# Expert mixer of a decoder layer: stored groups interleaved with direct ones, nine stored groups last, and new places for two sets of weights

## The chip, the cores and the metric

The kernel runs on one core of a Trainium2 chip. The metric is the device time of one execution in microseconds (us). A core has five engines that each work through a queue of their own in a fixed order: TensorE (PE; its weight loads are PEld), VectorE (DVE), ScalarE (ACT), GpSimd (POOL) and SyncE (SP, which only issues transfers here). Transfers of all queues run on the same 16 DMA engines.

## The reference, cut to what matters

One decoder layer for 1024 prompt tokens and 64 sample tokens, 1024 features wide: a token mixer, then an expert mixer (PEER), then a gated per-layer embedding (PLE) and a last norm. The change lies in the expert mixer and in the loading of the embedding's weights:

```python
# expert mixer: 16384 experts = 128 blocks of 128; 8 heads pick 16 experts each, so 128 per token
hval = jnp.einsum('pd,phkd->phk', xb, u_tab[e])
act = jax.nn.gelu(hval, approximate=False) * gsm
y = jnp.einsum('phk,phkd->pd', act, v_tab[e])
...
# per-layer embedding, which closes the layer
gate = jax.nn.sigmoid(rmsnorm(h, ple_norm) @ ple_gate)
h = h + gate * (p_l @ ple_proj)
```

## The kernel before

The tokens are nine tiles of 128 (the last, tile 8, holds the 64 sample tokens). The expert mixer treats them in two ways that run side by side.

**By gathers** (tiles 0, 1, 8, 2, 3; `gather`, L1161 to L1189). For each of a token's 128 experts POOL issues one indirect transfer that fetches a row of 1024 numbers per token (`grow`, 512 KB), first from the table of u, then from that of v. DVE takes each up with one instruction of 128x1024 elements: a product with the token's features and its sum for u (L1175), a weighted addition to `gacc` for v (L1189). Five buffers hold the fetched rows, so POOL can be at most five gathers ahead of DVE. There are 1152 gathers; tile 3 comes last, and its sum is added in the closing stage to the last tile's residual (L1447).

**Densely** (tiles 4 to 7, 512 tokens at once). For each block of 128 experts `hidden` loads 512 KB of u (`uraw`), splits it into a high and a low part (ACT L307, POOL L311), multiplies in 24 matmuls of 512 columns (L336, L337, L339) and applies the GELU; `act` multiplies with the gate weights (`wt`, one load of 448 KB for two blocks) and splits again (`ah`, `al`). `dense` then takes a group of blocks through eight output steps. A step loads its piece of v (`vraw`), splits it (`vh`, `vl`), does three matmuls per block into `py` (L1351, L1352, L1354) and adds the result to `yT` on DVE (L1358).

The hidden values of blocks 0 to 71 are computed in an earlier stage and stored in memory (`gd`); here they are called **stored** blocks, and the dense stage only loads them back (`ge`, 256 KB a block, two buffers). Blocks 72 to 127 are **direct**: their 24 hidden matmuls are done in the dense stage, between the steps of the group before. `dense_fused` runs the 14 direct groups of four blocks first, and `dense_stored` then the stored ones in 15 groups (14 of five blocks, one of two). While these run, `ple_weights` loads 20 pieces of the embedding's weights (`pgr`, 256 KB each, in buffers of the tag `vraw`) and splits them into the room that the tables of u have left; the last block of them has two buffers of its own (`pgx`). One piece is taken up every four steps (`PWS`).

**The closing stage** (`ple`) takes the nine tiles in the order 0, 1, 4, 5, 6, 7, 8, 2, 3: a norm, 60 matmuls with the embedding's weights, and the final norm (`fin`, L1490). Tile 3, the last, waits for the last gather.

No order is written out by hand. The code names the instructions in one sequence, with the gathers at a lower priority (`behind`), and a scheduler that models time turns it into one fixed list for each engine when the program is built. An engine never takes a later instruction of its list before an earlier one.

Of the kernel before, what the change touches and what calls it, by code (L numbers as in the profile page):

```python
# [9 lines left out]
F32 = mybir.dt.float32  # L10
F32R = mybir.dt.float32r
# [3 lines left out]
AF = mybir.ActivationFunctionType  # L15
# [149 lines left out]


CSTA = 288
NB = 5
GBUF = 5
UB = 2  # L170
PE_ = 0
# [2 lines left out]
PWS = 4  # L174
NPRE = 72
NF = 4
TK1 = {8: 0, 2: 1, 3: 4}
GEB = 2
GHB = 2
WQ = 32  # L180
VB = 4
WB = 2
AB = 8
CRING = 4
# [36 lines left out]
class K:  # L221
# [1116 lines left out]
    def dense(self, dl, dr, yT, groups, acts_of, side):  # L1338
        nc, I = self.nc, self.I
        for g0, nb in groups:  # L1340
            acts = acts_of(g0, nb)
            for d in range(8):
                next(side, None)
                raw = dl.tile([128, NB, 128], F32, name="vraw", bufs=VB)[:, :nb]
                nc.sync.dma_start(raw, I['pvd'][d, :, g0:g0 + nb])
                vh = dr.tile([128, NB, 128], F32R, name="vh")[:, :nb]
                vl = self.lo.tile([128, NB, 128], F32R, name="vl", bufs=2)[:, :nb]
                self.split(vh, vl, raw, "g")
# [9 lines left out]
                    nc.vector.tensor_tensor(yT[:, d, :], yT[:, d, :], p, op=OP.add)  # L1358
            self.first = False

    def dense_fused(self, dl, dr, hp, x, yT):

        groups = [(g, min(NF, 128 - g)) for g in range(NPRE, 128, NF)]
        made = {}

        def make(g):
            for b in range(g, min(g + NF, 128)):
                made[b] = self.act(dl, dr, b, self.hidden(hp, None, x, b))
                yield
                yield  # L1370

        for _ in make(NPRE):
            pass
        for g0, nb in groups:
            side = make(g0 + NF)
            self.dense(dl, dr, yT, [(g0, nb)], lambda g, n: [made.pop(b) for b in range(g, g + n)], side)
            for _ in side:
                pass

    def dense_stored(self, dl, dr, yT, side):  # L1380

        def acts(g0, nb):
            out = []
            for b in range(g0, g0 + nb):
                ge = dl.tile([128, self.ntok], F32, name="ge", bufs=GEB)
                self.nc.sync.dma_start(ge, self.gd[b])
                p = self.psh.tile([128, self.ntok], F32, name="ph")
                self.nc.scalar.activation(p, ge, AF.Copy)
                out.append(self.act(dl, dr, b, p))
            return out  # L1390

        def spread():
            while True:
                next(side, None)
                for _ in range(PWS):
                    yield

        self.dense(dl, dr, yT, [(g, min(NB, NPRE - g)) for g in range(0, NPRE, NB)], acts, spread())

    def ple_weights(self, cx, da, dl):  # L1400
        nc, I = self.nc, self.I
        kc = self.ntok // 128
        bufs = dict(uraw=UB, uh=DW, ul=LW, spare=1)
        names = [n for n in bufs for _ in range(bufs[n])]
        nc.sync.dma_start(self.pn, I['pnorm'])
        self.pg, self.pp = [], []
        for j in range(2):
            a = cx.tile([128, kc, 1024], F32R, name="pga", tag=f"cx{j}")
            self.pg.append([a[:, k] for k in range(kc)])
            self.pp.append([])  # L1410
# [9 lines left out]
        for w, src, n in ((self.pp, 'pproj', 2), (self.pg, 'pgate', 8)):  # L1420
            for k in range(n):
                for c in range(2):
                    cs = slice(c * 512, c * 512 + 512)
                    raw = dl.tile([128, 512], F32, name="pgr", tag="vraw", bufs=VB)
                    nc.sync.dma_start(raw, I[src][k, :, cs])
                    if src == 'pgate':
                        nc.scalar.activation(raw, raw, AF.Copy, scale=self.pn[:, k:k + 1])
                    self.split(w[0][k][:, cs], w[1][k][:, cs], raw, "g")
                    yield

    def ple(self, rp, tps, yT):
        nc, I, O = self.nc, self.I, self.O
# [3 lines left out]
        for i, t in enumerate(E0 + G2 + G1):  # L1436
# [50 lines left out]
            for c in range(2):  # L1487
                cs = slice(c * 512, c * 512 + 512)
                fin = rp.tile([128, 512], F32, name="fin", tag="vraw", bufs=VB)
                nc.vector.scalar_tensor_tensor(fin[:n], h[:n, cs], r[:n], gf[:n, cs], op0=OP.mult, op1=OP.mult)  # L1490
                nc.scalar.dma_start(O['y'][t * 128:t * 128 + n, cs], fin[:n])

    def build(self):
# [3 lines left out]
        with self.es:  # L1497
# [13 lines left out]
            a = self.group_a(pools, A0, "b", mixes)  # L1511
# [5 lines left out]
            a = self.group_a(pools, A1, "b")  # L1517
# [11 lines left out]
            a = self.group_a(self.a_pool(e2, "2"), A2, "b")  # L1529
# [4 lines left out]
            late = self.group_b(BORDER, early)  # L1534
# [10 lines left out]
            cx = sb("cx2", ex)  # L1545
            x = self.rows_of(cx, G2)
            da = sb("dna", eg, bufs=2)
# [17 lines left out]
            last = self.c_rows(co, late[-1], CRING, da, [y[:, :, n3:] for y in x])  # L1565
# [22 lines left out]
            yT = sb("dy", ey, side="right").tile([128, 8, self.ntok], F32, name="yT")  # L1588
# [3 lines left out]
            with ExitStack() as e:  # L1592
# [9 lines left out]
                for i, t in enumerate(G2 + [None]):  # L1602
                    tk = self.topk(tp, t) if t is not None else iter(())
                    while True:
                        a, b = next(tk, "end"), next(gate, "end")
# [13 lines left out]
            with ExitStack() as e:  # L1619
                dl = sb("dl", e, bufs=2)  # L1620
                with ExitStack() as e2:
                    self.psh = self.pool("psumh2", bufs=3, space=PS, es=e2, reuse_waits="tile")
                    self.ps2 = self.pool("psumy", bufs=3, space=PS, es=e2, reuse_waits="tile")
                    dr = sb("dr", e2, bufs=2)
                    self.dense_fused(dl, dr, da, x, yT)
                    self.dense_stored(dl, dr, yT, self.ple_weights(cx, da, dl))
# [23 lines left out]
```

## Time and profile before

| | |
|---|---|
| three timed runs | 3568.96, 3544.32 and 3556.01 us, median 3556.01 us |
| the profiled execution | 3571.98 us, its span 3570.2 us |
| first and last dense output matmul (`py`) | 2365.4 and 3405.2 us |
| PE busy, share of the span | 3218.4 us, 90% |
| DVE, POOL, ACT busy | 2801.1, 2330.2, 1177.6 us |
| moved by DMA | 1058.86 MB, mean 297 GB/s |

Times in rows are from the start of the span. The work before the dense stage fills about two thirds of the span. Shares of busy time are averages over stages with different limits, so the views by stretch and the waits say more than the table does.

### The profile page before, as it was taken

To read this page: it belongs to the slowest core of one execution; us is meant where nothing else is said; L and a number is where in the kernel's file an instruction comes from. 1 tells how busy PE (TensorE), PEld (TensorE's weight loads), DVE (VectorE), ACT (ScalarE), POOL (GpSimd) and SP (SyncE) were. 2 spreads that over 40 slices of the span, in tenths; PEclk is the share of its full clock that TensorE was granted. 3 is DMA by queue.
4 is the path that set the end of the run, shared out by engine and by line. 5 is a ranking of instruction groups with operands and counts; after the bars stand their busy time and mean duration, and the time that the engine had idled before them with its cause. 6 is when DMAs were issued, how large, how long until landed. Compare 5 with 4: busy or idle time off the path is not lost. (4 is left out here: it accounts for less than half of the span.)

```text
span 3570.2 us, 51592 instructions
## 1 busy us (share of the span) xinstructions
PE 3218.4 (90%) x17493; PEld 2663.8 (75%) x17493; DVE 2801.1 (78%) x5530; ACT 1177.6 (33%) x2255; POOL 2330.2 (65%) x2078
## 2 busy tenths in 40 slices
PE   7998995877869887879999999999999998899998
PEld 7897994654757666748877888878888886677775
DVE  4544589897797787879978899877777777788887
ACT  4332221111112111213235777743333333344322
POOL 5642577555345465545478787778888877788753
PEclk9999996656878787889999999999999999999999
DMA  8548599889857888896579888999999999999985
GB/s 267 173 136 272 188 314 327 274 311 323 299 179 267 286 296 277 290 351 228 196 270 311 330 323 334 345 348 343 340 344 339 341 333 371 352 377 385 343 276 203
DMA packets 416675, 1058.86 MB, mean 297 GB/s; under 512 B 45275, under 2 KB 140889, under 8 KB 411738
## 3 DMA queue, kind: packets, MB, share of 16 engines
q0 software_dynamic: 165888, 604.05, 47.2%
q1 hardware_dynamic: 198046, 364.18, 30.5%
q10 hardware_dynamic: 52476, 87.31, 6.6%
q8 instruction: 139, 2.28, 0.3%
q14 instruction: 126, 1.03, 0.1%
HBM read 968.09 MB, written 87.29 MB: 296 GB/s over the span
## 5 line engine op out<-in xcount | busy, mean ns | idle before, releaser
L1161 POOL DMA_INDIRECT grow<-in_pv,eid x576 | 566.2, 983 | 461.3 <-DVE gacc L1189 241.1
L1161 POOL DMA_INDIRECT grow<-in_pu,eid x576 | 560.8, 974 | 344.9 <-DVE grow L1175 218.4
L1175 DVE SCALAR_TENSOR_TENSOR grow<-grow,gacc 128x1024 f32<-128x1024 f32 x576 | 689.0, 1213 | 95.1 <-DMA grow<-in_pu,eid 92.5
L1189 DVE SCALAR_TENSOR_TENSOR gacc<-grow,ac,gacc 128x1024 f32<-128x1024 f32 x571 | 731.8, 1282 | 35.5 <-DMA grow<-in_pv,eid 29.1
L1351 PE MATMUL py<-ah,vh 128*128 128x512 f32 x1024 | 405.8, 397 | 23.2 <-ACT vh L307 20.9
L336 PE MATMUL ph<-cx,uh 128*128 128x512 f32 x1024 | 405.4, 396 | 6.2 <-ACT uh L307 6.1
L1352 PE MATMUL py<-al,vh 128*128 128x512 f32 x1024 | 404.7, 395 | 2.4 <-DVE al L309 2.2
L337 PE MATMUL ph<-cx,uh 128*128 128x512 f32 x1024 | 403.4, 394 | 0.0
L311 POOL TENSOR_TENSOR vl<-vraw,vh 128x512 fp32r<-128x512 f32 (+2 forms) x232 | 328.1, 1418 | 29.3 <-ACT vh L307 21.3
L311 POOL TENSOR_TENSOR ul<-uraw,uh 128x1024 fp32r<-128x1024 f32 x128 | 308.3, 2408 | 42.4 <-ACT uh L307 13.0
L1354 PE MATMUL py<-ah,vl 128*128 128x512 f32 x1024 | 278.0, 399 | 9.7 <-POOL vl L311 8.2
L339 PE MATMUL ph<-cx,ul 128*128 128x512 f32 x1024 | 263.6, 395 | 4.9 <-POOL ul L311 4.8
L1351 PEld LDWEIGHTS py<-ah,vh 128*128 128x128 f32 x1024 | 195.0, 190 | 73.6 <-ACT vh L307 28.5
L307 ACT ACTIVATE vh<-vraw 128x512 fp32r<-128x512 f32 (+2 forms) x232 | 156.0, 675 | 270.8 <-DMA vraw<-in_pvd 89.2
L1354 PEld LDWEIGHTS py<-ah,vl 128*128 128x128 f32 x1024 | 192.6, 190 | 61.1 <-POOL vl L311 17.5
L1358 DVE TENSOR_TENSOR yT<-yT,py 128x512 f32<-128x512 f32 x224 | 153.1, 684 | 105.3 <-PE py L1354 96.3
L336 PEld LDWEIGHTS ph<-cx,uh 128*128 128x128 f32 x1024 | 193.9, 189 | 49.2 <-ACT uh L307 8.9
L1352 PEld LDWEIGHTS py<-al,vh 128*128 128x128 f32 x1024 | 194.9, 190 | 45.5 <-DVE al L309 3.7
L339 PEld LDWEIGHTS ph<-cx,ul 128*128 128x128 f32 x1024 | 190.8, 189 | 44.7 <-POOL ul L311 6.8
L337 PEld LDWEIGHTS ph<-cx,uh 128*128 128x128 f32 x1024 | 193.6, 189 | 39.2
L307 ACT ACTIVATE uh<-uraw 128x1024 fp32r<-128x1024 f32 x128 | 135.0, 1055 | 158.9 <-DMA uraw<-in_puT 73.3
L311 POOL TENSOR_TENSOR wl<-wraw,wh 128x1024 fp32r<-128x1024 f32 x45 | 114.7, 2548 | 108.4 <-ACT wh L307 60.6
(420 smaller groups left out, 7041.4 us busy)
## 6 DMA issues: line engine op xcount, KB each, us to landing
uraw<-in_puT SPq DMA_DIRECT2D x128, 512.0 KB
vraw<-in_pvd SPq DMA_DIRECT2D x112, 320.0 KB
cw<-in_w_out SPq DMA_DIRECT2D x128, 256.0 KB
wd<-wst ACTq DMA_DIRECT2D x28, 1024.0 KB
wt<-wd SPq DMA_DIRECT2D x64, 448.0 KB
vraw<-in_pvd SPq DMA_DIRECT2D x112, 256.0 KB
wraw<-in_w_ret SPq DMA_DIRECT2D x48, 512.0 KB
wraw<-in_w_rw SPq DMA_DIRECT2D x42, 512.0 KB
```

The lines of the kernel that those rows point to most:

```text
L307: nc.scalar.activation(hi, src, AF.Copy)
L311: nc.gpsimd.tensor_tensor(lo, src, hi.bitcast(F32), op=OP.subtract)
L336: mm(out, lh(k), rh(k), start=first and k == 0, stop=False)
L337: mm(out, *((ll(k), rh(k)) if right else (lh(k), rl(k))), start=False, stop=False)
L339: mm(out, *((lh(k), rl(k)) if right else (ll(k), rh(k))), start=False, stop=last and k == nk - 1)
L1161: nc.gpsimd.indirect_dma_start(out=g, out_offset=None, in_=src, in_offset=bass.IndirectOffsetOnAxis(ap=self.eid[t][:, j:j + 1], axis=0))
L1175: nc.vector.scalar_tensor_tensor(g[:, c], g[:, c], 1.0, x[:, c], op0=OP.mult, op1=OP.mult, accum_out=hv[:, i, j:j + 1])
L1189: nc.vector.scalar_tensor_tensor(y[:, c], g[:, c], ac[:, j:j + 1], y[:, c], op0=OP.mult, op1=OP.add)
L1351: nc.tensor.matmul(p, vh[:, b, :], ah, start=b == 0, stop=False)
L1352: nc.tensor.matmul(p, vh[:, b, :], al, start=False, stop=False)
L1354: nc.tensor.matmul(p, vl[:, b, :], ah, start=False, stop=b == nb - 1)
L1358: nc.vector.tensor_tensor(yT[:, d, :], yT[:, d, :], p, op=OP.add)
```

## The change

The two functions become one, `dense_all`. All groups now have four blocks: 14 direct ones and 18 stored ones. The first nine stored groups are put between the direct ones (direct 72, direct 76, stored 0, direct 80, direct 84, stored 4 and so on by the first block's number); the other nine (`REST`) follow at the end. Each group's hidden values are prepared during the eight steps of the group before it, stored or direct alike. The embedding's weights are taken up during the last nine groups alone, one piece in three steps (`EVERY`). The raw loads of v get six buffers of four blocks in place of four of five. The raw weights move out of those buffers: all but the last block of them are loaded in one transfer of 512 KB into the two `pgx` buffers, one ahead, and the last block's own two tiles take that place when the raw loads have left it.

```diff
-NB = 5
+NB = 4
+REST = 9
+EVERY = 3
-VB = 4
+VB = 6
...
+    def dense_all(self, dl, dr, hp, x, yT, weights):
+        direct = list(range(NPRE, 128, NF))
+        stored = list(range(0, NPRE, NF))
+        beside = len(stored) - REST
+        order = []
+        for i, g in enumerate(direct):
+            order += [g] + stored[i * beside // len(direct):(i + 1) * beside // len(direct)]
+        order += stored[beside:]
+        made = {}
+
+        def make(g):
+            for b in range(g, g + NF):
+                if g < NPRE:
+                    ge = dl.tile([128, self.ntok], F32, name="ge", bufs=GEB)
+                    self.nc.sync.dma_start(ge, self.gd[b])
+                    h = self.psh.tile([128, self.ntok], F32, name="ph")
+                    self.nc.scalar.activation(h, ge, AF.Copy)
+                else:
+                    h = self.hidden(hp, None, x, b)
+                made[b] = self.act(dl, dr, b, h)
+                yield
+                yield
+
+        def both(a, b):
+            while True:
+                next(a, None)
+                next(b, None)
+                for _ in range(EVERY - 1):
+                    yield
+                    next(a, None)
+                yield
...
+        for i, g in enumerate(order):
+            side = make(order[i + 1]) if i + 1 < len(order) else iter(())
+            last = i >= len(order) - REST
+            self.dense(dl, dr, yT, [(g, NF)], lambda g0, nb: [made.pop(c) for c in range(g0, g0 + nb)], both(side, weights) if last else side)
+            for _ in side:
+                pass
+        for _ in weights:
+            pass
...
     def ple_weights(self, cx, da, dl):
...
-                        else:
-                            r[j].append(dl.tile([128, 1024], F32R, name="pgx", bufs=2))
...
+        def load(w, src, k):
+            if (w, k) in late:
+                raw = [dl.tile([128, 512], F32, name="pgr", tag="vraw", bufs=VB) for c in range(2)]
+                for c in range(2):
+                    nc.sync.dma_start(raw[c], I[src][k, :, c * 512:c * 512 + 512])
+            else:
+                raw = dl.tile([128, 2, 512], F32, name="pgr", tag="pgx", bufs=2)
+                nc.sync.dma_start(raw, I[src][k].rearrange("p (c d) -> p c d", c=2))
```

The lists of all engines are the same as before up to the start of the dense stage. (Two new lines of constants move the line numbers by two, and those behind `dense_all` by 24.) Three places in the lists show what moves.

On DVE, the end of the program before. `gacc` is the sum of tile 3's gathers, `fin` the last operation on a tile of the closing stage:

```order
L1482 SCALAR_TENSOR_TENSOR ph<-psg,ph 64x512
L1189 SCALAR_TENSOR_TENSOR gacc<-grow,ac,gacc 128x1024 x3
L1490 SCALAR_TENSOR_TENSOR fin<-ph,frs,row_norm_final 64x512 x2
L1481 SCALAR_TENSOR_TENSOR psg<-psg,ppp 128x512
L1189 SCALAR_TENSOR_TENSOR gacc<-grow,ac,gacc 128x1024
L1482 SCALAR_TENSOR_TENSOR ph<-psg,ph 128x512
L1189 SCALAR_TENSOR_TENSOR gacc<-grow,ac,gacc 128x1024 x2
L1447 TENSOR_TENSOR ph<-ph,gacc 128x1024
```

The same place of the changed program, from the last but one tile on:

```order
L1505 SCALAR_TENSOR_TENSOR psg<-psg,ppp 128x512
L1191 SCALAR_TENSOR_TENSOR gacc<-grow,ac,gacc 128x1024
L1506 SCALAR_TENSOR_TENSOR ph<-psg,ph 128x512
L1191 SCALAR_TENSOR_TENSOR gacc<-grow,ac,gacc 128x1024 x3
L1514 SCALAR_TENSOR_TENSOR fin<-ph,frs,row_norm_final 128x512 x2
L1191 SCALAR_TENSOR_TENSOR gacc<-grow,ac,gacc 128x1024 x42
L1471 TENSOR_TENSOR ph<-ph,gacc 128x1024
L311 TENSOR_TENSOR pxl<-ntr,pxh 128x512 x2
L1505 SCALAR_TENSOR_TENSOR psg<-psg,pyt 128x512
```

Before, the last gathers stand between the operations of tiles 8 and 2; now 42 of them stand alone between the end of tile 2 and the start of tile 3's norm.

On POOL, among the stored groups before, where `vl` is the split of v for one step, `pgb` one of the embedding's weights and `grow` a gather:

```order
L311 TENSOR_TENSOR vl_28619<-vraw_28616,vh_28618 128x640
L1161 DMA grow_21708<-in_pv,eid3_69 128x1024
L311 TENSOR_TENSOR vl_28642<-vraw_28639,vh_28641 128x640
L1161 DMA grow_21711<-in_pv,eid3_69 128x1024
L1161 DMA grow_21714<-in_pv,eid3_69 128x1024
L311 TENSOR_TENSOR pgb_26574<-pgr_28662,pgb_26573 128x512
L311 TENSOR_TENSOR vl_28670<-vraw_28667,vh_28669 128x640
L1161 DMA grow_21717<-in_pv,eid3_69 128x1024
L1161 DMA grow_21720<-in_pv,eid3_69 128x1024
L311 TENSOR_TENSOR vl_28693<-vraw_28690,vh_28692 128x640
```

And in the last nine groups of the changed program:

```order
L313 TENSOR_TENSOR vl_29114<-vraw_29111,vh_29113 128x512
L1163 DMA grow_21632<-in_pu,eid3_69 128x1024
L313 TENSOR_TENSOR vl_29139<-vraw_29136,vh_29138 128x512
L313 TENSOR_TENSOR vl_29171<-vraw_29168,vh_29170 128x512
L1163 DMA grow_21635<-in_pu,eid3_69 128x1024
L1163 DMA grow_21638<-in_pu,eid3_69 128x1024
L313 TENSOR_TENSOR vl_29191<-vraw_29188,vh_29190 128x512
L313 TENSOR_TENSOR vl_29224<-vraw_29221,vh_29223 128x512
L1163 DMA grow_21641<-in_pu,eid3_69 128x1024
```

There are fewer gathers for each step of v, and at this place tile 3 is still at its rows of u (`in_pu`) where before it was at those of v.

On SP, in the interleaved part of the changed program, before a stored group's turn (`uraw` belongs to the direct group that follows, `ge` and `wt` to the stored one and to both):

```order
L1315 DMA uraw_24272<-in_puT 128x1024
L1347 DMA vraw_23972<-in_pvd 128x512
L1347 DMA vraw_23992<-in_pvd 128x512
L1378 DMA ge_24012<-gd_15428 128x512
L1315 DMA uraw_24352<-in_puT 128x1024
L1378 DMA ge_24064<-gd_15428 128x512
L1347 DMA vraw_24024<-in_pvd 128x512
L1347 DMA vraw_24044<-in_pvd 128x512
L1331 DMA wt_24016<-wd_15427 128x7x128
L1331 DMA wt_24146<-wd_15427 128x7x128
```

Before, the direct groups' part of this list had only `uraw`, `vraw` and `wt`, and all but the first two loads of `ge` came behind it. Now loads for both kinds of block stand close together ahead of each stored group.

More of the change, by code (lines that the diff above doesn't have):

```diff
@@ L1359, in dense @@
             self.first = False
-    def dense_fused(self, dl, dr, hp, x, yT):
-        groups = [(g, min(NF, 128 - g)) for g in range(NPRE, 128, NF)]
+    def dense_all(self, dl, dr, hp, x, yT, weights):
[6 more added lines that the diff above has]
+        order += stored[beside:]
@@ L1364, in dense_fused @@
         made = {}
         def make(g):
-            for b in range(g, min(g + NF, 128)):
-                made[b] = self.act(dl, dr, b, self.hidden(hp, None, x, b))
+            for b in range(g, g + NF):
[7 more added lines that the diff above has]
+                made[b] = self.act(dl, dr, b, h)
@@ L1369, in make @@
                 yield
                 yield
-        for _ in make(NPRE):
-            pass
-        for g0, nb in groups:
-            side = make(g0 + NF)
-            self.dense(dl, dr, yT, [(g0, nb)], lambda g, n: [made.pop(b) for b in range(g, g + n)], side)
+        def both(a, b):
[6 more added lines that the diff above has]
+                yield
@@ L1377, in dense_fused @@
+        for _ in make(order[0]):
+            pass
+        for i, g in enumerate(order):
+            side = make(order[i + 1]) if i + 1 < len(order) else iter(())
+            last = i >= len(order) - REST
+            self.dense(dl, dr, yT, [(g, NF)], lambda g0, nb: [made.pop(c) for c in range(g0, g0 + nb)], both(side, weights) if last else side)
             for _ in side:
                 pass
[L1380 to L1398, printed above, removed]
+        for _ in weights:
+            pass
@@ L1417, in ple_weights @@
                             r[j].append(da.tile([128, 1024], F32R, name="pgb", tag=tag, bufs=bufs[tag]))
-                        else:
-                            r[j].append(dl.tile([128, 1024], F32R, name="pgx", bufs=2))
-        for w, src, n in ((self.pp, 'pproj', 2), (self.pg, 'pgate', 8)):
-            for k in range(n):
-                for c in range(2):
[L1423 to L1429, printed above, removed]
+        pieces = [(w, src, k) for w, src, n in ((self.pp, 'pproj', 2), (self.pg, 'pgate', 8)) for k in range(n)]
+        late = [(w, k) for w, src, k in pieces if len(w[0]) <= k]
+        raws = []
+        def load(w, src, k):
+            if (w, k) in late:
+                raw = [dl.tile([128, 512], F32, name="pgr", tag="vraw", bufs=VB) for c in range(2)]
+                for c in range(2):
+                    nc.sync.dma_start(raw[c], I[src][k, :, c * 512:c * 512 + 512])
+            else:
+                raw = dl.tile([128, 2, 512], F32, name="pgr", tag="pgx", bufs=2)
+                nc.sync.dma_start(raw, I[src][k].rearrange("p (c d) -> p c d", c=2))
+                raw = [raw[:, c] for c in range(2)]
+            raws.append(raw)
+        load(*pieces[0])
+        for i, (w, src, k) in enumerate(pieces):
+            if i + 1 < len(pieces):
+                load(*pieces[i + 1])
+            raw = raws.pop(0)
+            if (w, k) in late:
+                for j in range(2):
+                    w[j].append(dl.tile([128, 1024], F32R, name="pgx", bufs=2))
+            for c in range(2):
+                cs = slice(c * 512, c * 512 + 512)
+                if src == 'pgate':
+                    nc.scalar.activation(raw[c], raw[c], AF.Copy, scale=self.pn[:, k:k + 1])
+                self.split(w[0][k][:, cs], w[1][k][:, cs], raw[c], "g")
+                yield
     def ple(self, rp, tps, yT):
@@ L1624, in build @@
                     dr = sb("dr", e2, bufs=2)
-                    self.dense_fused(dl, dr, da, x, yT)
-                    self.dense_stored(dl, dr, yT, self.ple_weights(cx, da, dl))
+                    self.dense_all(dl, dr, da, x, yT, self.ple_weights(cx, da, dl))
                 ek.close()
```

## The prediction

> **What bounds the kernel now.** I read the busy time by stretch first: the interleaved direct part of the dense stage, its stored part, and the closing stage up to the end of the last but one tile. After the stretch and its length the columns are PE, PEld, DVE, ACT and POOL busy with counts, the granted clock, the DMA share and GB/s.
>
> ```profile
> 2365.00:2930.00 565.00, 565.00 (x2476) 464.48 (x2475) 429.62 (x614) 175.09 (x261) 479.80 (x392) 1.00 0.95 338
> 2930.00:3405.00 475.00, 439.66 (x1824) 345.50 (x1823) 384.96 (x625) 188.33 (x309) 386.13 (x326) 0.97 1.01 364
> 3405.00:3553.00 148.00, 133.51 (x612) 104.43 (x613) 120.49 (x132) 40.90 (x74) 75.65 (x93) 0.98 0.75 256
> ```
>
> and the 100 us of the stored part in which most was moved:
>
> ```profile
> 3200.00:3300.00 100.00, 94.29 (x401) 74.04 (x400) 83.04 (x119) 42.18 (x67) 83.94 (x69) 1.00 1.05 386
> ```
>
> While direct groups run, PE has no gap. While stored ones run it has, and the DMA share is at 1.01: PE has moved from bound to waiting. How much that costs comes from the pace of a full PE. The chain of waits holds one piece per hidden block while direct groups run, 33 pieces from this first to this last one; below them the first of an output step's three lines, with its first and last start:
>
> ```profile
> 2572.04 1.81 PE ph L339 x8
> ...
> 2922.76 1.81 PE ph L339 x8
> ...
> L1351 PE MATMUL py<-ah,vh x1024: 387/389/796, 2365.4 to 3404.0; 128*128 128x512 f32 x171
> ```
>
> They lie 350.72 / 32 = 10.96 us apart, and in each 10.96 us stand 24 hidden and 24 output matmuls: 0.2283 us a matmul. From 2365.4 to 3404.0 PE does 3 x 1024 output matmuls, but for the last few, and 13 direct groups x 96 hidden ones, some 4315 in all: 985 us of 1038.6. So **about 54 us** are lost, nearly all in the stored part. The waits of that part (who waited for whom: us, times, longest) say why:
>
> ```profile
> ACT vh L307 <- DMA vraw<-in_pvd: 89.2, 43, 7.2
> ...
> SPq L1345 <- POOL vl L311: 227.0, 97, 5.3
> ```
>
> The split of v, which PE needs, waits for its load, and the load's issue for one of the four buffers. The bytes agree. These are the sizes of one load:
>
> ```profile
> uraw<-in_puT SPq DMA_DIRECT2D x128, 512.0 KB
> vraw<-in_pvd SPq DMA_DIRECT2D x112, 320.0 KB
> ...
> wt<-wd SPq DMA_DIRECT2D x64, 448.0 KB
> vraw<-in_pvd SPq DMA_DIRECT2D x112, 256.0 KB
> ...
> ge<-gd SPq DMA_DIRECT2D x72, 256.0 KB
> ...
> pgr<-in_pgate SPq DMA_DIRECT2D x16, 256.0 KB
> ```
>
> The gathers come on top; by stretch (DVE and POOL busy with counts, clock, DMA share, GB/s) POOL issued 239, 175 and 53:
>
> ```profile
> 2365.00:2930.00 565.00, 296.60 (x350) 227.12 (x239) 1.00 0.95 338
> 2930.00:3405.00 475.00, 217.92 (x282) 166.93 (x175) 0.97 1.01 364
> 3405.00:3553.00 148.00, 72.67 (x57) 56.56 (x53) 0.98 0.75 256
> ```
>
> A stored group of five blocks wants 2.62 MB of v, 1.31 of `ge`, 1.15 of `wt`, 0.36 of embedding weights and 175 / 14.4 = 12.2 gathers of 0.524 MB (a row of 4 KB for 128 partitions), 11.8 MB in the 27.4 us that its 120 matmuls take: 432 GB/s, where 364 came. At 364 it takes 32.5 us, and 14.4 of them 468 of the 475 us. The stored part is bound by transfers, and more than half of these are gathers.
>
> The kernel's end hangs on the gathers too:
>
> ```profile
> 3536.33 3.94 DVE L1189 SCALAR_TENSOR_TENSOR gacc<-grow,ac,gacc 128x1024 f32<-128x1024 f32 x3 [0.97 <-DMA grow<-in_pv,eid]
> ...
> 3543.90 2.60 DVE L1189 SCALAR_TENSOR_TENSOR gacc<-grow,ac,gacc 128x1024 f32<-128x1024 f32 x2
> 3546.53 1.22 DVE L1447 TENSOR_TENSOR ph<-ph,gacc 128x1024 f32<-128x1024 f32 x1
> ...
> 3552.34 1.42 DVE L1490 SCALAR_TENSOR_TENSOR fin<-ph,frs,row_norm_final 128x512 f32<-128x512 f32 x2 [0.99 <-POOL frs L302]
> ```
>
> Tile 3's chain starts with L1447 at 3546.5, right behind the last gather, and takes the 23.7 us to 3570.2; tile 2 ends at 3553.8. So dense work and gathers end together now, and a change helps only if it shortens both.
>
> **The change part by part.** *Dense stage.* The interleaved part holds 14 direct and 9 stored groups, 807 us at PE's pace. A direct group moves 2.10 MB of u, 2.10 of v and 0.92 of `wt`; a stored one 2.10, 1.05 and 0.92. Counted in DVE's list, 302 gathers go beside them (681 stand ahead of the first addition to `yT`, 983 ahead of the 23rd group's end). That is 108 + 158 = 266 MB, 330 GB/s, below the 338 at which PE ran full. The nine last groups take 21.9 us each at PE's pace and want 4.07 MB, 0.58 of embedding weights and 66 / 9 = 7.3 gathers (3.84 MB): 8.5 MB, 388 GB/s. The best stretch above gave 386, the stored part 364; at 364 a group takes 23.3 us, a loss of 1.4 x 9 = 13 us. The short stretches before a stored group, in which PE has only output matmuls, want 7 to 10 gathers and 4.07 MB in 21.9 us, 353 to 425 GB/s. Unlike the stored part before, each stands behind a stretch of 43.8 us with less traffic, and v has six buffers for steps of 2.7 us. I put 3 us of the 54 on them. So the dense stage gives back 54 - 13 - 3 = **38 us**. Its ends are 0 (all stretches wait as the stored part did) and 54.
>
> *More steps.* Groups of four make 256 steps of the 232, so 24 more additions and splits:
>
> ```profile
> L1358 DVE TENSOR_TENSOR yT<-yT,py 128x512 f32<-128x512 f32 x224 | 153.1, 684 | 105.3 <-PE py L1354 96.3
> ```
>
> 24 x 0.684 = 16 us of DVE over 1000 us, beside PE's matmuls, whose number stays. I cost it at nothing; without the cover it would be 16 us. The weights of the embedding keep their bytes and splits, one transfer of 512 KB for two of 256 KB; nothing, as their last splits stand ahead of the last groups' end in POOL's list.
>
> *The gathers.* Fewer go beside the dense stage: behind its last addition DVE's list has 103, before 56. Five of the 47 stand among the closing stage's tiles, which PE fills to 133.5 of 148 us, at most 5 x 1.28 us; I take 2. The other **42 stand alone**, between the end of tile 2 and tile 3's chain. The trace has no such run, so I bound it. Below, DVE: three gathers back to back took 3.94 us, 1.31 each, 55 us for 42. Above, the five buffers: one is used again when its gather has landed and DVE is through, so five gathers take one landing plus 1.31 us and about 0.15 to the next issue. A short and a long landing for which DVE waited, as issue on POOL and use on DVE; the long one's use is the first row of the end above:
>
> ```profile
> 2899.12 0.96 POOL L1161 DMA_INDIRECT grow<-in_pu,eid  x1 [0.16 <-issue]
> ...
> 2903.66 1.22 DVE L1175 SCALAR_TENSOR_TENSOR grow<-grow,gacc 128x1024 f32<-128x1024 f32 x1 [1.36 <-DMA grow<-in_pu,eid]
> ...
> 3526.93 2.60 POOL L1161 DMA_INDIRECT grow<-in_pv,eid  x1 [0.17 <-DVE psg L1481]
> ```
>
> These are 4.5 and 9.4 us: (4.5 + 1.46) / 5 = 1.2, so DVE's 1.31 us a gather, or (9.4 + 1.46) / 5 = 2.2; for 42, 55 or 91 us. In the run nothing else moves and the first five have landed, so I take a value near the short row, 1.43 us, which is 367 GB/s: **60 us**. In front of it stand the 7.3 us by which tile 2 ends behind the last gather now.
>
> *PE goes cold.* After an idle gap, the matmuls of the closing stage come at this pace:
>
> ```profile
> 3419.25 1.97 PE L330 MATMUL ntr<-csta,ph 128*128 128x128 f32 x8 [3.98 <-DVE ph L1452]
> ...
> 3421.87 0.63 PE L336 MATMUL ppg<-pga,pxh 128*128 128x512 f32 x1
> 3422.30 0.63 PE L337 MATMUL ppg<-pga,pxh 128*128 128x512 f32 x1
> ```
>
> They start 0.43 us apart, near half pace, for some 5 us: 2.6 us lost. Behind the lone run tile 3 starts like that; 3 us.
>
> The sum, against the profiled execution's 3571.98 us (span 3570.2, 1.8 around it): -38 + 7 + 60 + 2 + 3 = **+34 us**, 3606. That execution is 16 us above the median of the runs, 3556.0; against the median it is 3590, 0.95% more.
>
> The Trainium skill, in DMA: Bandwidth & Descriptors, has two rules on this. Its section on the anatomy of a DMA on the GpSimd path puts one at about 2.0 us plus its bytes at 436 GB/s, 3.2 us for a gather here; the shortest row above is 4.5 us from issue to use. By that rule the lone run would go at DVE's pace, 55 us, and the sum would be +29; this is the first rival's price. Its section on specifications names about 358 GB/s from HBM for a core; by it the last groups' 8.5 MB would take 23.7 us, 16 us lost in place of 13, and the sum would be +37. The 386 GB/s row does not agree with it.
>
> **The rivals.**
>
> *The dense stage gives everything back and the run goes at DVE's pace.* -54 + 55 + 7 + 0 + 0 = +8 us, 3564: not slower. For it: 330 GB/s is under what the full PE stood, and the lone run has the DMA engines to itself. Against it: 388 GB/s in the last groups. It decides where those hold 386. 0.25.
>
> *The loads for the short stretches come late.* Four `ge` through two buffers, `wt` and the next group's u stand in one SP list with v, and the list stops at its first full buffer: 227 us of such waits stand above. If nine stretches lose 3 us each and the last groups wait like the stored part, the stage gives back 10 us, and a run at 1.6 us takes 67: -10 + 67 + 7 + 2 + 3 = +69 us, 3625, slower by 1.9%. For it: the bursts of 425 GB/s. Against it: the quieter 43.8 us ahead of each. 0.25.
>
> *Faster by over 1%* would take 36 us. PE's 54 us, and the 14.5 us that it idles in the closing stage, are less than 55 + 7 + 36. Only a gain ahead of the dense stage, where the lists are equal, could make it: 0.02. That the change does not interleave is excluded by the lists.
>
> **How the numbers follow.** Forecast (+34, from +20 to +50) 0.48, first rival 0.25, second 0.25, faster 0.02. A measurement of this kernel can tell about 1%, 36 us, from no change. The first rival and a little over half of the forecast lie within it: 0.25 + 0.27 = 0.52; the rest of the forecast and the second rival are slower: 0.21 + 0.25 = 0.46. The terms' ends give -54 + 55 + 7 = +8 to 0 + 91 + 7 + 6 + 3 = +107; a run at 2.2 us is unlikely beside idle DMA engines, so the range ends at +70, and begins at 0 for the spread of the runs: 3556 to 3626.
>
> **What would show it.** In the changed profile: no PE gap to speak of among the first 23 groups; the last output matmul about 38 us earlier, near 3367; DMA at 364 to 386 GB/s in the last nine groups; then, behind the end of tile 2, a stretch of some 60 us in which DVE does only L1191, POOL only L1163, and PE nothing; tile 3's first matmuls at half pace. I am wrong if that stretch is under 50 us, or if the gain ahead of it is over 54 or under 10.

## The result, and the profile after

The changed kernel takes 3587.94 us (median of four runs, 3581.34 to 3596.83) against 3555.71 us for the kernel before (four runs): the ratio on record is **1.0086, with a 95% interval from 1.0057 to 1.0116** (the quotient of the two medians is 1.0091). The forecast was 3590 us, in a range from 3556 to 3626. The profiled execution took 3581.34 us, its span 3579.6 us.

Busy time by stretch in the changed kernel, with the columns of the prediction: the dense stage up to the embedding's weights, while these are taken up, the last nine groups, the closing stage to the end of tile 2, and what follows up to tile 3's chain.

```profile
2347.00:3066.00 719.00, 718.52 (x3141) 589.76 (x3140) 546.35 (x841) 243.84 (x380) 596.92 (x493) 1.00 0.95 337
3066.00:3141.00 75.00, 71.42 (x305) 56.48 (x304) 56.93 (x105) 39.94 (x71) 67.82 (x61) 1.00 1.03 371
3141.00:3342.00 201.00, 197.95 (x858) 160.00 (x857) 166.34 (x273) 80.67 (x143) 163.01 (x146) 1.00 0.97 342
3342.00:3490.00 148.00, 128.03 (x587) 99.60 (x585) 125.29 (x136) 38.50 (x70) 83.38 (x101) 0.98 0.82 278
3490.00:3554.00 64.00, 0.00 (x0) 0.00 (x0) 53.93 (x42) 0.00 (x0) 35.31 (x38) 0.50 0.91 330
```

PE is full through the interleaved part (0.5 us of gaps in 719) and nearly so to the end of the dense stage. Behind the closing stage come 64 us in which PE does nothing. The wait for the loads of v, 89.2 us in the stored part before, has shrunk to this in the whole dense stage:

```profile
ACT vh L309 <- DMA vraw<-in_pvd: 4.7, 2, 2.9
```

The gathers alone, by stretch (DVE and POOL busy with counts; DVE has two instructions for a row of u, so the gathers are POOL's count): 370 issued beside the dense stage, 63 beside the closing stage, and 42 taken up by DVE behind it.

```profile
2347.00:3342.00 995.00, 456.49 (x587) 352.09 (x370) 1.00 0.96 341
3342.00:3490.00 148.00, 78.81 (x63) 64.51 (x63) 0.98 0.82 278
3490.00:3554.00 64.00, 53.93 (x42) 35.31 (x38) 0.50 0.91 330
```

The kernel's end on DVE, from the end of tile 2 to tile 3:

```profile
3488.44 1.41 DVE L1514 SCALAR_TENSOR_TENSOR fin<-ph,frs,row_norm_final 128x512 f32<-128x512 f32 x2
3489.77 3.93 DVE L1191 SCALAR_TENSOR_TENSOR gacc<-grow,ac,gacc 128x1024 f32<-128x1024 f32 x3
3494.67 1.29 DVE L1191 SCALAR_TENSOR_TENSOR gacc<-grow,ac,gacc 128x1024 f32<-128x1024 f32 x1 [0.97 <-DMA grow<-in_pv,eid]
...
3550.03 3.94 DVE L1191 SCALAR_TENSOR_TENSOR gacc<-grow,ac,gacc 128x1024 f32<-128x1024 f32 x3 [0.24 <-DMA grow<-in_pv,eid]
3554.00 1.22 DVE L1471 TENSOR_TENSOR ph<-ph,gacc 128x1024 f32<-128x1024 f32 x1
```

From 3489.8 to 3554.0 DVE does 42 additions of 1.29 us, with waits of 0.2 to 1.1 us for a gather between them: 64.2 us, 1.53 a gather. Tile 3's chain then takes 25.6 us to the span's end.

The two profiled spans differ by only 9.4 us, less than the medians do. The dense stage began 18.5 us earlier in the profile after (2346.7 against 2365.2), although all lists are equal up to there. In the seven profiles of kernels that have nothing changed ahead of it (before, after and the first five experiments below) it began anywhere from 2346.7 to 2370.5. So stages are compared from their own start here: from the first `py` (its weight load included) to the span's end 1205.0 us before and 1232.9 after, 27.9 more; the medians differ by 32.2.

### The profile page after: what moved, and what is told of

It is laid out like the page before. It is cut to its first block, busy times and chain, and to the rows that moved or that the text cites. A ratio compares the mean times of both kernels' runs of the same rounds, so it can differ in the third digit from the quotient of the medians.

```text
span 3579.6 us, 51796 instructions
## 1 busy us (share of the span) xinstructions
PE 3204.7 (90%) x17493; PEld 2661.9 (74%) x17493; DVE 2819.8 (79%) x5554; ACT 1177.7 (33%) x2279; POOL 2330.6 (65%) x2102
## 2 busy tenths in 40 slices
DMA packets 418835, 1058.86 MB, mean 296 GB/s; under 512 B 45515, under 2 KB 140105, under 8 KB 413898
## 5 line engine op out<-in xcount | busy, mean ns | idle before, releaser
L313 POOL TENSOR_TENSOR vl<-vraw,vh 128x512 fp32r<-128x512 f32 x256 | 331.7, 1300 | 61.6 <-ACT vh L309 33.5
L309 ACT ACTIVATE vh<-vraw 128x512 fp32r<-128x512 f32 x256 | 161.3, 631 | 353.8 <-PE py L1354 219.1
L1360 DVE TENSOR_TENSOR yT<-yT,py 128x512 f32<-128x512 f32 x248 | 169.7, 685 | 133.8 <-PE py L1356 132.2
L341 PEld LDWEIGHTS ph<-cx,ul 128*128 128x128 f32 x1024 | 190.1, 188 | 43.3 <-POOL ul L313 5.4
```

The source lines that it names most:

```text
L309: nc.scalar.activation(hi, src, AF.Copy)
L313: nc.gpsimd.tensor_tensor(lo, src, hi.bitcast(F32), op=OP.subtract)
L341: mm(out, *((lh(k), rl(k)) if right else (ll(k), rh(k))), start=False, stop=last and k == nk - 1)
```

## The experiments

Two theories stood against each other. **A**, the forecast's: interleaving and the deeper buffers win back PE's time in the dense stage, and the lone run of gathers takes it away again; without that run the gain is there to be had. **B**: transfers bind this half of the kernel, the sum of bytes is the same (1058.86 MB), and the dense stage became shorter mostly because its gathers were put off; the order of the groups hardly matters.

All runs in one table. "Beside" are the gathers that POOL issued from the first to the last `py`, "MB" what moved in that time (both counted in the trace), "lone" the time from the end of tile 2 to the last gather's addition, with the gathers that DVE's list has there. A dash: the gathers ended before tile 2 did. "Single run": timed once, so without a ratio. The stage times come from one profile of each kernel; the four with 362 to 371 gathers beside the dense stage and six buffers for v lie within 6 us of each other (993.9 to 999.8), so differences of that size say nothing. e9 and e10 do 72 more matmuls in the dense stage than the others (16 us, see below).

| kernel | dense us | PE gaps us | beside | MB | closing us | lone us (gathers) | ratio to before |
|---|---|---|---|---|---|---|---|
| before | 1040.2 | 35.3 | 415 | 364 | 148.1 | - | 1 |
| after | 994.9 | 7.1 | 370 | 339 | 148.0 | 64.1 (42) | 1.0086 [1.0057, 1.0116] |
| e1_without_42 | 999.8 | 10.3 | 370 | 339 | 147.1 | 1.2 (0) | 0.9913 [0.9884, 0.9942] |
| e2_four_buffers | 1042.2 | 35.3 | 395 | 352 | 150.6 | 21.7 (14) | 1.0093 [1.0053, 1.0133] |
| e3_three_buffers | 1078.5 | 60.9 | 421 | 366 | 138.3 | - | 1.0080 [1.0048, 1.0113] |
| e4_six_in_old_order | 1011.9 | 18.3 | 388 | 349 | 141.7 | 32.2 (21) | 1.0025 [0.9999, 1.0050] |
| e5_no_interleave | 1012.4 | 18.0 | 384 | 346 | 140.5 | 41.1 (27) | 1.0054 [1.0031, 1.0078] |
| e6_six_gather_buffers | 1018.7 | 19.6 | 392 | 350 | 140.5 | - | 1.0165 [1.0125, 1.0205] |
| e7_six_gather_buffers_old_order | 1106.2 | 79.8 | 424 | 370 | 131.0 | - | 1.0412 [1.0372, 1.0453] |
| e8_four_gather_buffers | 993.9 | 5.6 | 362 | 335 | 153.2 | 105.2 (58) | single run |
| e9_six_with_room_in_yT | 1040.9 | 22.9 | 400 | 359 | 141.1 | - | 1.0021 [0.9996, 1.0047] |
| e10_same_without_interleave | 1062.4 | 35.7 | 427 | 372 | 142.0 | - | 1.0040 [1.0016, 1.0065] |
| e11_one_store_buffer | 998.6 | 8.2 | 371 | 339 | 144.0 | 43.3 (28) | single run |

**e1_without_42: the lone run taken away.** The changed kernel without the last 42 of tile 3's v rows.

```diff
         y = home()
+        n = n - 42 if t == G1[-1] else n
         for j in range(n):
```

> The changed kernel without the last 42 gathers of tile 3's rows of v (their part of the sum is left out); all lists are otherwise as in the changed kernel, and no gather stands alone any more. Theory A (the dense stage gained about 45 us and the lone run takes it back and more): 3588 - 42 x 1.53 = about 3524 us, that is 32 us under the kernel before, with the last output matmul about where it is in the changed kernel. Theory C (the changed kernel is slow for another reason, such as late loads in the short stretches; the lone run only fills time that would be lost anyway): less than 40 us off, over 3548.

Measured: 3537.91 us against 3570.5 us for the kernel before, timed beside it, ratio 0.9913. Tile 3's sum lacks these rows; only the time of the run is of use. Against the change's own ratio this is 1.0086 - 0.9913 = 1.73%, 62 us, where the profile gives the lone run 64. The dense and the closing stage stayed as they were (999.8 and 147.1 us). The price of the lone run is shown; not what put it there.

**e2_four_buffers and e3_three_buffers: the buffers of v undone, the new order kept.**

```diff
-VB = 6
+VB = 4      # e3: 3
```

> The changed kernel with four raw buffers for v in place of six. In DVE's list 76 gathers are then left behind the dense stage (103 with six, 56 before) and 14 stand alone (42 with six). Theory A (interleaving leaves room, so that gathers beside the dense stage are nearly free): the lone run falls by 28 x 1.53 = 43 us, the last nine groups pay 5 to 10: about 3553 us, equal to before. Theory B (transfers are the bound everywhere, and a gather moved beside the dense stage costs its 0.524 MB at about 364 GB/s, 1.44 us, there): -43 + 27 x 1.44 = -4, about 3584 us.

> The changed kernel with three raw buffers for v. 52 gathers are left behind the dense stage and none stands alone. Theory A: -42 x 1.53 - 7 for the lone run and what stands ahead of it, +15 to 30 for 51 more gathers beside the dense stage at 386 GB/s and for PE waiting on three buffers: 3532 to 3547 us, faster than before. Theory B: -71 + 51 x 1.44 = +2, about 3590 us. If three buffers starve PE, the last output matmul comes later than in the kernel before.

Measured: 3609.6 and 3599.2 us against 3570.5, ratios 1.0093 and 1.0080, both as slow as the change. The lone run shrank from 64 us to 22 and to nothing, and the dense stage grew by 47 and 84 us. The last nine groups in the two, first with four, then with three buffers:

```profile
3177.00:3411.00 234.00, 212.72 (x867) 167.56 (x868) 191.54 (x288) 79.12 (x139) 179.79 (x164) 0.96 0.96 338
```

```profile
3166.00:3431.00 265.00, 220.98 (x862) 169.68 (x861) 212.04 (x298) 78.85 (x137) 196.54 (x182) 0.92 0.96 335
```

DMA moves no more in a microsecond than in the changed kernel (342 GB/s) while PE waits 21 and 44 us. It also moves less than the 364 GB/s of the stored part before, so these waits are not for a transfer rate alone: with three or four buffers of four blocks the loads of v may themselves be asked for too late. The two effects, more gathers and fewer buffers, are not parted by these runs. With fewer buffers for v the list that the scheduler builds holds more gathers in the dense stage: behind the last addition to `yT` DVE's list has 103 of them with six buffers, 76 with four, 52 with three. What the lone run gave back, the dense stage took. Theory A's expectations, level with before for four buffers and faster for three, fell; B's 3584 and 3590 us, 1.008 and 1.010 of its 3556, are near what came. The last output matmul of three buffers came later than before (1078.5 us behind the first, not 1040.2), which was the sign for a starved PE.

**e4_six_in_old_order and e5_no_interleave: the buffers without the interleaving.** The first is the kernel before with groups of four and six buffers; the second is the changed kernel with all stored groups at the end.

```diff
# e4, in the kernel before
-NB = 5
+NB = 4
-VB = 4
+VB = 6
# e5, in the changed kernel
-REST = 9
+REST = 18
```

> The kernel before with groups of four and six raw buffers for v, and nothing else: all direct groups first, the old weights' loads. DVE's list then leaves 84 gathers behind the dense stage (56 before) and 21 stand alone at the end. If the interleaving is what gave the dense stage its 45 us, the stored part stays as long as before and the run of 21 comes on top: 3556 + 7 + 32 = 3595 us. If the six buffers and the fewer gathers beside the stage gave them, the stored part shortens by about 28 x 1.44 = 40 us and the sum is 3556 + 39 - 40 = 3555 us.

> The changed kernel with all 18 stored groups behind the 14 direct ones (REST 18 in place of 9), so without the interleaving, with six buffers and the new weights' loads. 90 gathers are left behind the dense stage and 27 stand alone (103 and 42 with the interleaving, 56 and 0 before). Theory B (transfers bound this half of the kernel, so where the dense loads stand changes little): the stored part shortens by about 34 x 1.44 = 49 us against the kernel before, the lone run costs 27 x 1.53 + 7 = 48: level with before, ratio 0.997 to 1.005, and about 0.5% under the changed kernel. Theory A (the interleaving gives the dense stage its 45 us): the stored part stays, ratio 1.01 to 1.02.

Measured: 3578.84 us against 3570.5 (1.0025) and 3589.14 against 3569.86 (1.0054). The dense stage took 1011.9 and 1012.4 us: **28 of the 45 us that it gained come without any interleaving**. The stored part of e4:

```profile
2958.00:3383.00 425.00, 406.75 (x1731) 324.26 (x1730) 349.65 (x584) 177.33 (x312) 346.36 (x308) 0.99 1.00 353
```

and that of e5:

```profile
2928.00:3373.00 445.00, 427.05 (x1816) 340.39 (x1815) 363.98 (x619) 183.57 (x321) 357.25 (x317) 0.99 0.99 348
```

PE loses 18 us in each where it lost 35 in the stored part before, and the DMA rate is below the 364 GB/s of then. That fits a PE that waits less because less is asked: in e4 27 gathers fewer stand beside the dense stage. (The six buffers alone, at an equal number of gathers, were not tried.) In e5 there are 31 fewer. Of these 21 and 27 stand alone behind tile 2, for 32.2 and 41.1 us. With the interleaving come the other 17 us of the dense stage, and 21 and 15 more lone gathers. A in its strong form, that the new order makes the gain, is refuted. B comes nearer in both, though e5's 1.0054 lies just above its range (0.997 to 1.005), and e5 is 0.3% under the changed kernel instead of 0.5%.

**e6_six_gather_buffers, e7_six_gather_buffers_old_order and e8_four_gather_buffers: what sets the lone run.** A sixth buffer for gathered rows, with room from one buffer fewer for stored hidden values, for a small tile and (e6) for v. Then the opposite, four.

```diff
-GBUF = 5
+GBUF = 6      # e8: 4, and nothing else
-GHB = 2
+GHB = 1
-        it = wp.tile([128, 128], F32, name="it", bufs=2)
+        it = wp.tile([128, 128], F32, name="it", bufs=1)
...
# e6 starts from the changed kernel (VB = 5), e7 from the kernel before (NB = 4)
```

> The changed kernel with six buffers for gathered rows in place of five and five raw buffers for v in place of six (one buffer fewer for stored hidden values and for one small tile makes the room). The scheduler then puts 42 more gathers ahead of the dense stage (723 stand ahead of its first addition, 681 before) and leaves 40 behind it, none alone. Ahead of the dense stage DMA ran at 297 GB/s, 0.83 busy, so there the 22 MB cost little; in the dense stage the last nine groups take 82 gathers, with five buffers about 1.5 us each over 66: 225 us. 1019 us for the dense stage, 148 for the closing stage, 13 behind it, 1180 against 1202 before: ratio 0.99 to 0.995 if the stage ahead takes its gathers for nothing, 1.01 if they cost 1.44 us each there too.

> The kernel before with six buffers for gathered rows, groups of four, and the same room made; nothing of the interleaving or the new weights' loads. 725 gathers stand ahead of the dense stage's first addition and none is left behind the stage. If where the gathers stand decides and the interleaving does not, this is about as fast as the changed kernel with six: the stored part takes 45 more gathers than before (65 us more at 1.44), but 42 fewer stand in the rest and the closing stage, now free of 56 of them, loses its waits for them (about 15 us): ratio 0.99 to 1.01. If the dense stage cannot take more gathers at that rate, 1.02.

> The changed kernel with four buffers for gathered rows in place of five. 121 gathers are left behind the dense stage and 58 stand alone. The lone run's pace by the buffers: a landing of 6.1 us and 1.46 us to the next issue over four buffers, 1.9 us a gather, 110 us for the run (it took 1.53 us a gather with five). If the DMA engines set the pace and not the buffers, it stays at 1.5 us, 88 us.

Measured, four buffers (a single run): 58 lone gathers in 105.2 us, 1.81 each, with only these at work (DVE and POOL busy with counts):

```profile
3521.00:3626.00 105.00, 74.43 (x58) 51.50 (x55) 0.50 0.85 285
```

So **the buffers set the pace of the lone run**, 1.53 us with five and 1.81 with four. The trace has 6.0 us as the median from issue to landing in the lone run of the changed kernel:

```profile
grow<-in_pv,eid POOLq DMA_INDIRECT x38, 6.0
```

(6.0 + 1.29 + 0.15) / 5 = 1.49 and / 4 = 1.86, near both. The trace of e8 holds no landing times, so the second figure is an estimate with the first one's landing. The rival, a pace set by the DMA engines, would have left it at 1.5 us.

Six buffers: 3623.55 us against 3569.86 (1.0165) and 3710.64 (1.0412), both far above what was expected. First, in both the dense stage begins late, at 2451.7 and 2459.8, over 80 us behind the latest of the seven above; the room taken from the stores has a large part in it (e11, below). In the stage ahead of it, in e6, the first row among the waits is

```profile
ACT geh L1322 <- DMA gd<-geh: 93.7, 31, 6.6
```

The GELU of a stored block now waits until the one before has been written out. Behind the start of its dense stage e6 is as forecast: 1174.4 us to the span's end, 1180 expected and 1205.0 before. What it gains there it loses, and more, ahead of it, where 42 more gathers and the shorter room stand. Second, e7 has all gathers done by 3473.7, beside the dense stage, which takes 1106 us for it and leaves the closing stage with idle transfers:

```profile
3030.00:3567.00 537.00, 457.25 (x1818) 349.88 (x1817) 413.65 (x610) 190.78 (x329) 394.02 (x355) 0.95 0.91 328
3567.00:3697.00 130.00, 128.88 (x612) 103.07 (x611) 53.82 (x76) 41.10 (x74) 17.30 (x40) 1.00 0.23 72
```

PE loses 80 us in the upper row and DMA rests in the lower. From the start of its dense stage e7 takes 1252.3 us, 47 more than before. My expectation that all gathers beside the dense stage would be about level is refuted.

**e9_six_with_room_in_yT, e10_same_without_interleave and e11_one_store_buffer: the same without that room.** Six gather buffers and five of v, while the stored hidden values wait in slices of `yT`, which is not yet in use; e10 is this without interleaving; e11 is the changed kernel with the single store buffer, and the single buffer for the small tile `it`, alone.

```diff
# e9 (and e10, with REST = 18)
-GBUF = 5
+GBUF = 6
-VB = 6
+VB = 5
-        ge = ep.tile([128, self.ntok], F32, name="geh", bufs=GHB) if ep else p
+        ge = ep[:, i1 % 8] if ep is not None else p
...
# e11
-GHB = 2
+GHB = 1
-        it = wp.tile([128, 128], F32, name="it", bufs=2)
+        it = wp.tile([128, 128], F32, name="it", bufs=1)
...
```

> The kernel with six gather buffers and five raw buffers for v again, but the room is made otherwise: the stored blocks' hidden values go to memory from the eight slices of yT, which is idle in that stage, so two buffers become eight instead of one. 701 gathers stand ahead of the dense stage's first addition, 60 are left behind the stage, none alone. If the 86 us that the kernel with six buffers lost ahead of the dense stage came from its single buffer for stored values (ACT waited 93.7 us for the store there), the dense stage starts where it did before, and 1019 + 148 + 13 = 1180 us behind that start against 1202 give a ratio of 0.99 to 0.997, faster than both kernels. If they came from 42 more gathers in that stage, half of them are still there: the start comes 30 to 45 us later and the ratio is 1.00 to 1.01.

> The same with all 18 stored groups behind the direct ones. 34 gathers are left behind the dense stage, 60 with the interleaving; so the stored part takes 167 gathers in 18 groups. If where the dense loads stand changes little (theory B), the sum is level with the interleaved one within 0.5%. If the interleaving is worth something once no gather stands alone, it is slower than the interleaved one by more than that: 26 more gathers beside the dense stage at 1.44 us, 37 us, less what the closing stage gains, some 15 us: ratio 1.00.

> The changed kernel with five gather buffers and six for v as it is, but one buffer for stored hidden values (two in the changed kernel) and one for a small tile of the gate weights. If the single buffer is what delayed the dense stage, it starts 60 to 90 us later than the 2347 us of the changed kernel, at about 2420; if six gather buffers delayed it, it starts at about 2350.

Measured: e11 (a single run) starts its dense stage at 2408.8, 62 us later than the changed kernel and 38 us behind the latest of the seven, and has 103.5 us of the wait for the store where e6 had 93.7. The second line is that of the kernel before, with two buffers:

```profile
ACT geh L1322 <- DMA gd<-geh: 103.5, 34, 8.0
```

```profile
ACT geh L1320 <- DMA gd<-geh: 15.0, 3, 7.4
```

So the smaller room costs 38 to 62 us. That it is the store buffer and not `it` is read from the waits; e11 undoes both at once. It also has 12 more gathers ahead of the dense stage than the changed kernel (695 and 683 issued), but e9 has as many (696) and begins at 2341.6, or at some 2358 with the 16 us of matmuls added that it leaves for later. e9 has no lone run and takes 3561.58 us against 3553.25: 1.0021 [0.9996, 1.0047], level with before and 0.65% under the change, but not under 1 as expected. Its dense stage took 1040.9 us instead of 1019. In it, as in e10, PE did some 4370 matmuls where the others have some 4300: hidden matmuls of three blocks stand behind the first `py`, 72 x 0.2283 = 16 us of work that was done ahead before. Against the changed kernel's 994.9 us the other 30 us go with 30 gathers more, which show in its last nine groups:

```profile
3164.00:3384.00 220.00, 207.32 (x873) 163.00 (x873) 190.88 (x267) 78.97 (x140) 178.86 (x164) 0.98 0.98 353
```

e10: 3567.92 us, 1.0040; 427 gathers beside the dense stage, 62 us between the last gather and the end of tile 2, and a closing stage at 183 GB/s. Interleaving here is worth 0.2%, within the two intervals and, as theory B had it, under 0.5%.

No kernel of this study is shown to be faster than the one before, but for e1, which leaves work out.

## Why the prediction was right

The forecast's sum was +34 us against the profiled execution; by the stages of the two profiles it is -45 + 7 + 64 + 0 + 2 = +28, and by the medians +32. Both large terms were somewhat too small, the gain by 7 us and the lone run by 4; that these errors have opposite effects and nearly cancel is luck. The mechanism, a fuller PE in the dense stage and then a stretch of gathers alone, is what the trace shows and e1 prices. Step by step:

*PE without gaps in the first 23 groups: right but for the embedding's weights.* 0.5 us of gaps in 719 us; 3.6 us in the 75 us ahead of 3141, for the reason in the next point. The 3 us for the short stretches were right as a bound. One reason given for it was not: the 807 us at PE's pace hold the hidden matmuls of the first direct group, which stand ahead of the dense stage. By the 4315 matmuls of the prediction's own sum it is 985 - 9 x 21.9 = 788 us, and its 266 MB are 338 GB/s, no longer below the rate at which PE ran full. The 794 us measured moved 340 GB/s, and PE stayed full all the same.

*38 us from the dense stage: 45 measured.* Of these, 28 us are gaps of PE that went (35.3 to 7.1), and 17 us are PE's busy time, 1005.1 to 988.0 us for the same some 4300 matmuls: its granted clock in the stored part was 0.97, and it is 1.00 in all three stretches of the dense stage now. The prediction's 54 us, reckoned by PE's pace, hold both. (The last output matmul starts at 3341.4, not near 3367; 18.5 us of that are the earlier start.) The term that was too large is the 13 us for the last nine groups. They took 22.3 us each, not 23.3, and DMA ran at 342 GB/s, not at 364 to 386: the demand of 8.5 MB a group was overstated. The loads of the embedding's weights say where:

```profile
L1436 SPq DMA_DIRECT2D pgr<-in_pgate x7: 328/328/1158, 3066.2 to 3130.2; - x7
L1433 SPq DMA_DIRECT2D pgr<-in_pgate x2: 328/328/328, 3240.4 to 3242.8; - x2
```

The code names them beside the last nine groups, but the list has all but the last two small ones ahead of these (the 23rd group ends at 3140.8). (Two more, of 512 KB each, go out at 2320.5, even ahead of the dense stage.) That takes most of the 0.58 MB a group from the sum. Also the last group has no successor to load `ge` and `wt` for, 1.97 MB or 0.22 a group. So some 7.7 of the 8.5 MB remain; 201 us at 342 GB/s are 7.6 a group.

*42 gathers at 1.43 us, 60 us: 64.2 measured, 1.53 each.* The lower bound, DVE's pace (55), and the upper one, five buffers with a landing of 9.4 us (91), held. The landing was 6.0 us in the median, between the 4.5 and 9.4 of the two rows; I had leaned on the short one because nothing else moves there. The Trainium skill, in DMA: Bandwidth & Descriptors, section on the anatomy of a DMA on the GpSimd path, has a rule, a fixed time plus the bytes at a rate, from which I estimated 3.2 us for such a gather; by that estimate even four buffers would keep DVE busy. The 6.0 us here and the 1.81 us a gather of e8 disagree with it.

*5 gathers among the closing tiles, 2 us: nothing measured.* The closing stage took 148.0 us, before 148.1. Its DMA rose from 254 to 278 GB/s, beside PE.

*7.3 us from tile 2's end to the last gather's place:* right; the last gather's addition ended 7.3 us ahead of tile 2 before, and 64.1 us behind it after.

*PE cold for tile 3, 3 us: 1.9.* Tile 3's chain took 25.6 us for 23.7. Its first matmuls after the run:

```profile
3555.37 1.94 PE L332 MATMUL ntr<-csta,ph 128*128 128x128 f32 x8 [73.56 <-DVE ph L1471]
...
3558.16 0.63 PE L338 MATMUL ppg<-pga,pxh 128*128 128x512 f32 x1
3558.59 0.63 PE L339 MATMUL ppg<-pga,pxh 128*128 128x512 f32 x1
...
3562.01 0.39 PE L338 MATMUL ppg<-pga,pxh 128*128 128x512 f32 x1
3562.24 0.40 PE L339 MATMUL ppg<-pga,pxh 128*128 128x512 f32 x1
```

They start 0.43 us apart up to 3561.2 and 0.23 behind it: ten at 0.2 us lost. The Trainium skill, in TensorE: Matmul & The Clock Gate, Part 1, says that the clock falls to half after a window of some 3.4 us idle and comes back about as long into steady work. The granted clock of 0.50 in the lone run and the step at 3561.2, 5.8 us behind the first matmul, agree with the halving; the way back is somewhat longer here. (In the other five kernels with a lone run of 14 gathers or more the step comes 4.3 to 5.6 us behind the first matmul.)

*24 more additions and splits, 16 us of DVE, at nothing:* the dense stage came out shorter than forecast, with DVE busy for 770 of its 995 us, so nothing speaks for a cost.

What the forecast did not see is what its own numbers already held. It costed 38 us of gain and 60 of loss as separate effects of the change. They are largely one effect, seen at two places: the dense stage gave up 45 gathers, 23.6 MB of its 25 MB less. The queues of the dense stage, of gathers (`q0`) and of the loads, before and then after:

```profile
q0 software_dynamic: 59709, 217.44, 56.2%
q1 hardware_dynamic: 109140, 145.17, 41.1%
```

```profile
q0 software_dynamic: 53243, 193.86, 53.0%
q1 hardware_dynamic: 110135, 143.69, 42.9%
```

The thirteen kernels fit that reading in the main: 334 to 350 GB/s over the dense stage, 994 to 1000 us with 371 gathers or fewer beside it, 1012 to 1019 with 384 to 392, 1040 to 1106 with 395 or more. Within the last group the count does not decide. With 395 gathers e2 took as long (1042 us) as the kernel before with 415 (1040), and e7 took 44 us longer than e10 with three gathers fewer. The stored part of e10, which has five buffers for v, moved 365 GB/s, as the kernel before did, where e7 with four had 328:

```profile
2943.00:3415.00 472.00, 439.10 (x1819) 340.39 (x1818) 406.93 (x632) 180.59 (x322) 388.00 (x350) 0.99 1.01 365
```

So few buffers for v seem to lengthen the stage on their own; no run varied them at a fixed number of gathers.

What a gather costs beside the dense stage, then, is known only roughly. By its bytes at 350 GB/s it would be 0.524 MB / 350, or 1.50 us, where transfers bind (an estimate). The pairs of rows in which the buffers for v stay at the same number (after and e4, after and e5, e9 and e10, all with five or six) give 0.8 to 1.3 us a gather; after against e2 and e3 gives 1.9 and 1.6, with the buffers' share in it. Alone a gather costs 1.53. So moving gathers behind the dense stage gains little or nothing, and once PE has no gaps left (988 us busy) it is a pure loss. Beside the closing stage a gather costs least: the stage is 131.0 us long with none (e7) and 148.0 with 63, about 0.3 us each.

Open: why the transfers do not go faster in the dense stage, when 386 GB/s stood for 100 us before; and whether a list with more gathers in the interleaved part (337 GB/s, PE full) and none alone would win. No kernel here had such a list. Each number of buffers for v gave another number of gathers in the lists (103, 76 and 52 left behind the dense stage with six, four and three); that the scheduler's modelled times are the reason was not tested.

## What to carry to other kernels

When a stage becomes shorter after a change, count what moved in it before and after: if its bytes fell with its time, work may have been put off, and it must be looked for in front of the stage and behind it. Where a scheduler builds the lists, the buffers given to one stream can change how much of another stays beside it; read the count of each stream per stage in the new lists before costing a wait that goes. A run of transfers that stands alone went at the pace of its buffers here, (landing + use) / buffers, so look for a place for it where PE works and DMA rests.

## What the runs showed of the hardware

Five gathers of 512 KB in flight, with nothing else of weight moving, land 6.0 us after issue in the median, as against 6.2 us for the rows of u among all the traffic of the first 23 groups, so the lack of other traffic hardly made them faster (the DMA share in the run was still 0.91):

```profile
grow<-in_pu,eid POOLq DMA_INDIRECT x176, 6.2
```

The lone run moved 330 GB/s with five buffers and 285 with four, no more than the dense stage with all its queues (334 to 350).

Behind an idle stretch of 31 us or more PE's matmuls start 0.43 us apart and then, 4.3 to 5.8 us behind the first one, 0.23; six kernels with a lone run show it.
